# Twelve conditioning steps as blocks of 256 columns behind the small products of the heads

## The chip, the cores and the metric

The kernel runs on one core of a Trainium2 chip. The metric is device time in microseconds (us) of one execution. Five engines work side by side, each through its own list of instructions in order: TensorE (PE) multiplies, VectorE (DVE) and ScalarE (ACT) do elementwise work, GpSimd (POOL) a little of it, and SyncE (SP) issues most of the transfers (DMA) from memory.

## The reference, cut to what matters

One decoder layer on 520 tokens (a prompt of 512 and 8 samples of one token), width 1024. All is computed in float32.

```python
cs  = silu(c)                                   # one conditioning row for the prompt, 8 for the samples
mod = cs @ w_mod + b_mod                        # w_mod [1024, 6144]: six parts of 1024 columns
sh1, sc1, g1, sh2, sc2, g2 = split(mod, 6)      # parts 0 to 5
h = rmsnorm(x, norm1_g) * (1 + sc1) + sh1
u = h @ w_in                                    # q, f, i, og, xb, yb, ga, gb: 8 x 1024 columns
o_a = rmsnorm(hgrn2(q, f, i, S0)) * silu(og)    # 8 heads of 128, chunkwise recurrence
o_b = rglru(conv(xb)) * gelu(yb)
merged = sigmoid(ga) * (o_a @ w_branch_a) + sigmoid(gb) * (o_b @ w_branch_b)
x = x + g1 * (merged @ w_out)
h2 = rmsnorm(x, norm2_g) * (1 + sc2) + sh2
x = x + g2 * (square(relu(h2 @ w_ff1)) @ w_ff2)
y = rmsnorm(x, final_norm_g)
```

Parts 2 (g1), 3 (sh2), 4 (sc2) and 5 (g2) of mod are needed only from the out-projection on. They are what the change moves.

## The kernel before

Tokens lie along the columns in two halves of 260. Each 128 columns of a weight matrix are a tile of 1024x128 float32, 512 KB, which SP loads into one of four buffers of the pool `wst` (`_load_w`, L106; L104 for rows of w_mod). ACT casts it to fp32r (`whi`, L115), DVE subtracts to get the rest (`wlo`, L118), and PE makes 48 products of 128x260 from a tile (`products`, L157): 8 blocks of K, three combinations of high and low halves, two halves of the tokens. These are called the main products below. The buffer of a tile is free when DVE has made `wlo` from it.

`run` writes a list of steps, each with its weights and a function. `weights`, `ready_w` and `take_w` turn the list of weights into the order of loads and splits, some tiles ahead of their use. A scheduler then places the instructions of each engine by the times it reckons for them, by priorities (`urgent`, `together`) and by ties set by hand (`behind`). So the code's order isn't the program's order; that is read from the built program.

The heads come first. Two heads make a pair, (0,1), (2,3), (4,5), (6,7). For each head the tiles kf, kq, kg and kv are multiplied; for each odd head `heads_prompt` works out the products within chunks of the pair by levels b = 1, 2, 4, ..., 64. A level is 32 small products in narrow columns of PE (128x32 stationary; moving 64 wide at b=1, L661, 32 wide from b=2 to 16, L666; 16 products at b=32; 8 of 64x64 at b=64, L670, with the sample products L619 behind them). After each level DVE multiplies the operands X for the next (L682 four times after b=1, L678 twice after each other one), so a level waits for DVE, and main products stand between the levels. DVE also makes the RG-LRU recurrence (`rg_scans`) in that time. Then come the gates, the two branches, the out-projection and the MLP.

Conditioning parts 0 and 1 are made in a start-up block. Parts 2, 4, 3 and 5 are made in 16 steps: a step takes two blocks of 128 rows of w_mod, 1024 columns wide (two loads of 512 KB, not split), and makes 8 products of 128x32 by 128x256 in float32 (`mod_rows`, L403), summed in PSUM over four steps. After a part's fourth step ACT copies the sum (`mod_out`), and two products with an identity (`mod_cols`, L417) and an addition on DVE turn it into columns. `mod_step` puts one step behind each gate with j = 5, others after branch tiles by a share, and one after every second tile of the out-projection.

Of the kernel before, what the change touches and what calls it, by code (L numbers as in the profile page):

```python
# [6 lines left out]
F32 = mybir.dt.float32  # L7
# [4 lines left out]
OP = mybir.AluOpType  # L12
# [3 lines left out]
D = 1024  # L16
# [4 lines left out]
KO = D // 128  # L21
# [13 lines left out]
FIRSTS = 3  # L35
ROWS = "rows"
MARK = "mark"
PLAIN = 8
# [41 lines left out]
class Kernel:  # L80
# [19 lines left out]
    def _load_w(self, key, pool):  # L100
        src, r0, c0 = key[:3]
        st = pool.tile([128, KO, 128], F32, name="wst")
        if ROWS in key:
# [295 lines left out]

    def mod_rows(self, ps, k, w):  # L400

        for j in range(4):
            self.nc.tensor.matmul(ps[32 * j:32 * j + 32, :256], self.cT[:, k, :], w[:, 256 * j:256 * j + 256],  # L403
                                  start=k == 0, stop=k == KO - 1)

# [22 lines left out]
    def mod(self, part, k):  # L428

        w = [self.take_w(self.mod_key(part, k + n)) for n in range(2)]  # L430
        if k == 0:
            self.psm = self.ppt.tile([128, 512], F32, name="pt")
        for n in range(2):
            self.mod_rows(self.psm, k + n, w[n])
        if k == KO - 2:
            self.mod_open = part, self.modT[:, 8 * part:8 * part + 8], self.mod_out(self.psm), \
                self.n2g if part == 4 else None

    def modc(self, part, k):
# [103 lines left out]

    def head(self, h, first=None):
# [4 lines left out]
        q = self.head_q(X[:, 2], first[1] if first else self.gemm(kq, self.h)[:, :, :HALF])  # L549
        og = self.slot(self.hg, "e")  # L550
        if first:
# [80 lines left out]
    def heads_prompt(self, hs):  # L632
# [5 lines left out]
        a32 = self.hg.tile([128, 2, NC, 32], F32, name="a32", bufs=1)  # L638
        at = self.at

        def halves(x, b, n):
# [8 lines left out]
        while b < C:  # L650
            n = L // (2 * b)
            p = self.pps.tile([128, 512], F32, name="ps")
            with self.together():
                for e in range(2):
                    Q, K = X[:, e, 0], X[:, e, 1]
                    for c in range(NC):
                        if b == 1:
                            for j in range(4):
                                s, o = c * C + 32 * j, 256 * e + 64 * c
                                o = p[32 * j:32 * j + 32, o:o + 64].rearrange("p (x t) -> p x t", x=2)  # L660
                                nc.tensor.matmul(o, K[:, s:s + 32], X[:, e, 0::2, s:s + 32], start=True, stop=True)  # L661
                        elif b <= 32:
                            for j in range(0, 128, 32 if b < 32 else 64):
                                s, o = c * C + j, 128 * e + 32 * c
                                d = s if b < 32 else s + 32
                                nc.tensor.matmul(p[j:j + 32, o:o + 32], K[:, s:s + 32], Q[:, d:d + 32], start=True,  # L666
                                                 stop=True)
                        else:
                            s, o = c * C, 256 * e + 64 * c
                            nc.tensor.matmul(p[:64, o:o + 64], K[:, s:s + 64], Q[:, s + 64:s + 128], start=True,  # L670
                                             stop=True)
                if b == 64:
                    po = self.heads_sample(hs)
# [1023 lines left out]
    def run(self):  # L1697
# [28 lines left out]
        def mod_step(due):  # L1726
            if due < 0.999 or not mods:
                return due
            p, k = mods.pop(0)
            steps.append(([self.mod_key(p, k + n) for n in range(2)], self.mod, p, k))  # L1730
            return due - 1

# [3 lines left out]
        for h in range(H):  # L1736
            kf, kq, kv, kg = self.head_cols(h)
            steps.append(([kf, kq, kg, kv][FIRSTS if h == 0 else 0:], self.head_start if h == 0 else self.head, h))
# [16 lines left out]
        self.gate_out = {"a": ga, "b": gb}  # L1755
        share, due = (len(mods) - n - 2) / (2 * KO), 0.0
        last = len(self.gate_seq) - 1
        marks = [s for s, (u, j) in enumerate(self.gate_seq) if j in (1, 2)][:-1] + [last - 3, last - 1]
        for s, (u, j) in enumerate(self.gate_seq):
# [3 lines left out]
            if j == 5:  # L1763
                mod_step(1)
        steps.append(([], self.end_gates))
        tiles = [("b", m) for m in range(KO)] + [("a", m) for m in range(KO)]
        for g, m in tiles:
# [4 lines left out]
            else:  # L1772
                one("w_branch_a", m, lambda m: self.merge(m, ga.pop(m), gb.pop(m)), m)
            due = mod_step(due + share)
        steps.append(([], self.load_xT))
        steps.append(([], self.shifts))
        steps.append(([], self.begin_strassen))
        for m in range(KO):
            one("w_out", m, self.out_proj, m)
            if m % 2:  # L1780
                mod_step(1)
        assert not mods, mods
        steps.append(([], self.norm2))
# [306 lines left out]
```

## Time and profile before

| | |
|---|---|
| runs | 1012.15, 1014.35, 1015.53 us, median 1014.35 |
| profiled execution | 1014.92 us, its span 1013.1 us |
| PE, DVE, ACT, POOL busy | 993.7, 709.8, 529.4, 136.2 us |
| heads | about 60 to 442 us |
| gates | about 442 to 491 us |
| branches, out-projection | about 491 to 630 us, then the MLP |

All durations in the prediction are of the profiled execution; its own time stands 0.57 us above the median of the runs. In the groups of the profile a row has the line, the engine, the operation, out<-in, the shapes and the count, then busy time, the mean of one in ns, and the idle time just before it with what ended it. In the timeline a row has start and length in us. A matmul's length includes its way through the array, so matmuls that follow each other overlap, and what one costs the stream is read from starts. [...]

### The profile page before, as it was taken

The page shows a single profiled execution, that of the slowest core. Times are in us where ns is not written, and L with a number is a line of the kernel's source. Part 1 is how long each engine was busy: PE and PEld are TensorE (multiplying, and loading weights), DVE is VectorE, ACT ScalarE, POOL GpSimd, SP SyncE. Part 2 cuts the span into 40 slices and gives each one's busy share as a digit, 9 for nine tenths or more (in the row PEclk, how much of TensorE's full clock was granted, in tenths as well). Part 3 has the DMA queues.
Part 4 walks back from the last instruction along what each step waited for, and adds up shares of the span by engine and source line. Part 5 has one row for each costly group of instructions (what it writes and reads, how often), then busy time and mean ns, then how long its engine had stood idle before and what let it go on. Part 6 is the DMA issues. An engine that isn't in the chain of part 4 may idle for free. (4 is left out here: it accounts for less than half of the span.)

```text
span 1013.1 us, 23612 instructions
## 1 busy us (share of the span) xinstructions
PE 993.7 (98%) x9690; PEld 962.5 (95%) x9690; DVE 709.8 (70%) x1489; ACT 529.4 (52%) x1007; POOL 136.2 (13%) x261
## 2 busy tenths in 40 slices
PE   6999999999999999999999999999999999999997
PEld 5799999999989999998999999999999999999996
DVE  7586767695676669987723646667767776777685
ACT  6374645744663564455512224466555645646663
POOL 4220000000000000111100000022321331242050
PEclk7999999999999999999999999999999999999999
DMA  9883354345335435548357876332772483274242
GB/s 298 272 250 111 112 147 130 102 121 140 112 110 147 125 98 160 156 156 255 116 170 216 269 223 188 104 85 50 151 176 64 98 196 103 53 165 97 64 84 85
DMA packets 205278, 145.81 MB, mean 144 GB/s; under 512 B 6979, under 2 KB 193755, under 8 KB 205162
## 3 DMA queue, kind: packets, MB, share of 16 engines
q1 hardware_dynamic: 193586, 127.43, 43.0%
q0 software_dynamic: 11568, 16.84, 7.7%
q8 instruction: 76, 1.25, 0.5%
q14 instruction: 32, 0.26, 0.1%
q10 hardware_dynamic: 16, 0.03, 0.0%
HBM read 123.61 MB, written 13.39 MB: 135 GB/s over the span
## 5 line engine op out<-in xcount | busy, mean ns | idle before, releaser
L157 PE MATMUL mm<-h,whi 128*128 128x260 f32 (+1 forms) x2688 | 446.9, 285 | 0.0
L157 PEld LDWEIGHTS mm<-h,whi 128*128 128x128 f32 x2688 | 374.2, 189 | 1.5 <-issue 0.6
L157 PE MATMUL mm<-h,wlo 128*128 128x260 f32 x1344 | 276.5, 285 | 1.1 <-DVE wlo L118 1.1
L118 DVE TENSOR_TENSOR wlo<-wst,whi 128x1024 fp32r<-128x1024 f32 x156 | 190.5, 1222 | 113.4 <-ACT whi L115 108.0
L115 ACT CAST whi<-wst 128x1024 fp32r<-128x1024 f32 x156 | 163.5, 1050 | 187.7 <-PE mm L157 141.7
L157 PEld LDWEIGHTS mm<-h,wlo 128*128 128x128 f32 x1344 | 209.7, 189 | 2.2 <-DVE wlo L118 1.5
L916 POOL DMA_DIRECT2D t<-obT_d x8 | 4.3, 544 | 371.1 <-DVE g L745 365.5
L1421 DVE TENSOR_TENSOR f<-f 128x260 f32<-128x260 f32 x64 | 27.3, 427 | 27.9 <-ACT f L1416 27.2
L1413 POOL TENSOR_TENSOR ft<-ft,fsh 128x8 f32<-128x8 f32 x28 | 18.5, 659 | 207.4 <-DVE ft L1407 207.4
L1410 ACT ACTIVATE ft<-ft,fsh 128x512 f32<-128x512 f32 (+2 forms) x36 | 24.1, 676 | 36.0 <-DVE ft L1407 36.0
L157 PE MATMUL mm<-oa,whi 128*128 128x260 f32 x256 | 41.9, 285 | 0.0
L157 PE MATMUL mm<-a,whi 128*128 128x260 f32 x256 | 41.5, 284 | 0.0
L157 PE MATMUL mm<-b,whi 128*128 128x260 f32 x256 | 41.3, 284 | 0.0
L157 PEld LDWEIGHTS mm<-oa,whi 128*128 128x128 f32 x256 | 34.9, 188 | 2.1 <-ACT whi L115 1.2
L157 PEld LDWEIGHTS mm<-a,whi 128*128 128x128 f32 x256 | 35.0, 188 | 1.2 <-PE pt L403 0.8
L157 PEld LDWEIGHTS mm<-b,whi 128*128 128x128 f32 x256 | 34.9, 188 | 1.2 <-issue 0.8
L678 DVE TENSOR_TENSOR X<-X,tb 128x512 f32<-128x512 f32 x48 | 30.9, 685 | 4.1 <-PE ps L670 3.0
L1455 POOL DMA_DIRECT2D ma<-snap x28 | 27.6, 1001 | 38.5 <-issue 25.3
L1437 POOL DMA_DIRECT2D ma<-snap x28 | 27.0, 965 | 40.7 <-DMA ma<-snap 25.5
L1416 ACT ACTIVATE f<-ft 128x520 f32<-128x520 f32 (+1 forms) x36 | 20.8, 588 | 15.0 <-POOL ft L1414 13.0
L586 ACT ACTIVATE st<-st,fkq 128x128 f32<-128x128 f32 x64 | 19.8, 393 | 14.7 <-DMA st<-in_state_hgrn_dram 11.1
L1002 DVE TENSOR_TENSOR wgate<-gw,wgate 128x512 fp32r<-128x512 f32 x28 | 19.0, 689 | 11.1 <-ACT wgate L1001 11.0
(623 smaller groups left out, 2144.3 us busy)
## 6 DMA issues: line engine op xcount, KB each, us to landing
wst<-in_w_in_dram SPq DMA_DIRECT2D x56, 512.0 KB, 4.3
wst<-in_w_mod_dram SPq DMA_DIRECT2D x32, 512.0 KB, 4.1
wst<-in_w_ff_dram SPq DMA_DIRECT2D x64, 256.0 KB, 4.1
wst<-in_w_ff_dram SPq DMA_DIRECT2D x32, 512.0 KB, 5.1
wm<-in_w_mod_dram SPq DMA_DIRECT2D x8, 1024.0 KB, 10.7
st<-in_state_hgrn_dram SPq DMA_DIRECT2D x8, 512.0 KB, 6.8
vb<-vd SPq DMA_DIRECT2D x8, 512.0 KB, 3.8
out_dram<-st SPq DMA_DIRECT2D x8, 512.0 KB, 3.2
```

Of the source, the lines that this page charges most:

```text
L115: ins = self.nc.scalar.copy(hi, st)
L118: self.nc.vector.tensor_tensor(lo, st, hi.bitcast(F32), OP.subtract)
L157: self.last_product = self.nc.tensor.matmul(ps[s][:, :c.stop - c.start], x, y[:, c], start=first and n == 0, stop=last and n == 2)
L586: nc.scalar.activation(st[:, b], st[:, b], AF.Copy, scale=fkq[:, b:b + 1])
L678: last = nc.vector.tensor_tensor(half, half, factors(tbs, x, b), OP.mult)
L1002: nc.vector.tensor_tensor(lo, x, hi.bitcast(F32), OP.subtract)
L1410: nc.scalar.activation(t[:, :p], t[:, :p], AF.Relu, bias=sh[:, 0:1])
L1413: eng.tensor_tensor(t[:, p:], t[:, p:], sh[:, 1:9], OP.add)
L1416: nc.scalar.activation(f, self.two(self.ft)[:, a:a + n], AF.Square)
L1421: self.nc.vector.tensor_tensor(f[:, n], f[:, a], f[:, b], op)
L1437: nc.gpsimd.dma_start(x[1][:, b], v[:, :n], accum_op=OP.add)
L1455: nc.gpsimd.dma_start(x[t][:, a], s[p], accum_op=OP.add)
```

## The change

Parts 2, 4 and 3 become twelve units (`mod_unit`): four blocks of 256 columns for each part, each with all of K. A unit's weights are two tiles of 1024x128, loaded like other tiles (512 KB each) and not split; they keep their two buffers until the unit's last product. A unit makes 32 products of 128x32 by 128x64 (L459), a copy on ACT, two products of 128x64 by 64x18 (L468) and one or two operations on DVE (L475, L477). Its products are tied behind the last product of a level, `level_last[b]`, with b from `UNITS`. Three pairs have four units each: in pairs (0,1), (2,3) and (4,5) a unit stands after the odd head (b=1), one after the two rg_y tiles (b=4), one in the next even head after q (b=16) and one after that head (b=64). They are called U0 to U3, U4 to U7 and U8 to U11 here. Part 5 keeps its four steps, all behind the gates with j = 5. `ready_w` counts loaded tiles that are still held, instead of places in the list.

```diff
+UNITS = (1, 4, 16, 64)
...
-            while self.wnext_load < min(self.wnext_split + loads, len(self.worder)):
+            while self.wnext_load < len(self.worder) and self.staged() < loads:
...
+    def staged(self):
+        return max(sum(st is not None for st in self.wstage.values()), self.wnext_load - self.wnext_split - 8)
...
+    def mod_unit(self, u, b):
+
+        nc, (part, n) = self.nc, u
+        w = [self.take_w(key).rearrange("p (k n) -> p k n", k=KO) for key in self.unit_keys(u)]
+        pt = self.ppb.tile([128, 512], F32, name="pb")
+        with self.together():
+            for k in range(KO):
+                for j in range(4):
+                    x, e = divmod(j, 2)
+                    ins = nc.tensor.matmul(pt[32 * j:32 * j + 32, :64], self.cT[:, k, :],
+                                           w[e][:, k, 64 * x:64 * x + 64], start=k == 0, stop=k == KO - 1)
+                    self.behind(ins, self.level_last[b])
+        ev = self.sm.tile([128, 256], F32, name="modev")
+        with self.urgent():
+            nc.scalar.copy(ev[:, :64], pt[:, :64])
+        own = self.ident.rearrange("p (j c) -> p j c", c=32)[:, :, :NM]
+        with self.together():
+            for x in range(2):
+                ins = nc.tensor.matmul(pt[64 * x:64 * x + 64, 64:64 + 2 * NM].rearrange("p (e b) -> p e b", b=NM),
+                                       ev[:, :64], own[:, 2 * x:2 * x + 2], start=True, stop=True)
+                if 2 * b in self.level_last:
+                    self.behind(ins, self.level_last[2 * b])
...
-        mods = [(p, k) for p in (2, 4, 3, 5) for k in range(0, KO, 2)]
+        units = [(p, n) for p in (2, 4, 3) for n in range(4)]
+        mods = [(5, k) for k in range(0, KO, 2)]
...
+            if h and h % 2 == 0:
+                u = units[:2]
+                del units[:2]
+                steps.append(([kf, kq, *self.unit_keys(u[0]), kg, kv], self.head, h, None, u[0]))
+                steps.append((self.unit_keys(u[1]), self.mod_unit, u[1], UNITS[3]))
+            else:
+                steps.append(([kf, kq, kg, kv][FIRSTS if h == 0 else 0:], self.head_start if h == 0 else self.head, h))
+            if h % 2 and h < H - 1:
+                u = units.pop(0)
+                steps.append((self.unit_keys(u), self.mod_unit, u, UNITS[0]))
             for n in (h - 1, h) if h % 2 else (h, h + 1):
                 one("w_in", (40 if h % 2 else 32) + n, self.rg_y if h % 2 else self.rg_x, n)
+            if h % 2 and h < H - 1:
+                u = units.pop(0)
+                steps.append((self.unit_keys(u), self.mod_unit, u, UNITS[1]))
...
-            due = mod_step(due + share)
...
-            if m % 2:
-                mod_step(1)
```

The order of instructions shows where this lands. First, PE at the levels b=1 and b=2 of pair (2,3). L157 is a main product, L661 the level b=1, L628 transposes, L666 a level from b=2 on. Before:

```order
L661 MATMUL ps<-X_799 32x64 x32
L157 MATMUL mm<-h,whi 128x260 x2
L628 MATMUL pt<-ident,X_798 128x128 x4
L157 MATMUL mm<-h,wlo 128x260 x2
L157 MATMUL mm<-h,whi 128x260 x4
L157 MATMUL mm<-h,wlo 128x260 x2
L157 MATMUL mm<-h,whi 128x260 x4
L157 MATMUL mm<-h,wlo 128x260 x2
L666 MATMUL ps<-X_799 32x32 x32
```

After, where L704 is the level b=1, L710 a level from b=2 on, L162 a main product and L459 a product of U4:

```order
L704 MATMUL ps<-X_799 32x64 x32
L459 MATMUL pb<-wst,cT 32x64 x19
L710 MATMUL ps<-X_799 32x32 x16
L459 MATMUL pb<-wst,cT 32x64
L710 MATMUL ps<-X_799 32x32 x16
L459 MATMUL pb<-wst,cT 32x64 x12
L162 MATMUL mm<-h,whi 128x260
```

The 16 main products between the two levels are gone from there; 19 unit products stand in their place, and the rest of U4 stands around the halves of b=2.

Second, PE around the level b=16 of the same pair. Before, 37 main products stand between b=8 and b=16 and 33 behind it; a piece:

```order
L157 MATMUL mm<-h,whi 128x260 x4
L157 MATMUL mm<-h,wlo 128x260 x2
L157 MATMUL mm<-h,whi 128x260 x2
L666 MATMUL ps<-X_799 32x32 x32
L157 MATMUL mm<-h,whi 128x260 x2
L157 MATMUL mm<-h,wlo 128x260 x2
```

After, from the level b=8 to U6 (L468 are the column products of U5):

```order
L710 MATMUL ps<-X_799 32x32 x32
L459 MATMUL pb<-wst,cT 32x64 x23
L162 MATMUL mm<-h,whi 128x260 x4
L162 MATMUL mm<-h,wlo 128x260 x2
L162 MATMUL mm<-h,whi 128x260 x4
L162 MATMUL mm<-h,wlo 128x260 x2
L162 MATMUL mm<-h,whi 128x260 x4
L162 MATMUL mm<-h,wlo 128x260 x2
L162 MATMUL mm<-h,whi 128x260 x4
L468 MATMUL pb<-ident,modev 64x18 x2
L710 MATMUL ps<-X_799 32x32 x32
L459 MATMUL pb<-wst,cT 32x64 x32
```

Between b=8 and b=16 stand 23 products of U5, 22 main products and two column products; U6 follows b=16 directly, and 18 main products stand between it and b=32. From b=1 to b=64 the pair has 209 main products before and 151 after. On DVE the split of kf's tile stands in the new order directly ahead of the two operations L723 that make X after b=8, with two copies and one operation of the RG-LRU between them.

Third, the transfers that SP issues in that stretch, with what each waits for. Before:

```order
L776 DMA oaT_d_95<-e_1252 128x512 [waits DVE_49]
L106 DMA wst_3226<-in_w_in_dram 128x8x128 [waits DMAHW6_49,DVE_49]
L610 DMA out_5_dram<-st_2415 128x8x128 [waits DMAHW7_49,DVE_49]
L106 DMA wst_3286<-in_w_in_dram 128x8x128 [waits DMAHW0_49,DVE_49]
L885 DMA obT_d_96<-y_3150 128x520 [waits DMAHW1_49,DVE_49]
L106 DMA wst_3344<-in_w_in_dram 128x8x128 [waits DVE_49]
```

After, where wst_3307 is the second tile of U5, wst_3371 kf's and wst_3373 kq's tile of the next head, wst_3375 and wst_3480 the two tiles of U6, and wst_3540 kg's:

```order
L108 DMA wst_3307<-in_w_mod_dram 128x8x128 [waits PE_49]
L108 DMA wst_3371<-in_w_in_dram 128x8x128 [waits DMAHW7_49,PE_49]
L652 DMA out_5_dram<-st_2583 128x8x128 [waits DMAHW0_49,DVE_49]
L108 DMA wst_3373<-in_w_in_dram 128x8x128 [waits DMAHW1_49,DVE_49]
L108 DMA wst_3375<-in_w_mod_dram 128x8x128 [waits DMAHW7_49,DMAHW2_49,DVE_49]
L108 DMA wst_3480<-in_w_mod_dram 128x8x128 [waits PE_49]
L108 DMA wst_3540<-in_w_in_dram 128x8x128 [waits DMAHW6_49,DMAHW4_49,PE_49]
```

Before, each load waits for the split of an earlier tile. After, wst_3307 and wst_3371 wait for the last product of U4 on PE, wst_3375 for the split of kf's tile on DVE, and wst_3480 and wst_3540 for the end of U5.

More of the change, by code (lines that the diff above doesn't have):

```diff
@@ L36 @@
 ROWS = "rows"
+UNIT = "unit"
+UNITS = (1, 4, 16, 64)
 MARK = "mark"
@@ L102, in _load_w @@
         st = pool.tile([128, KO, 128], F32, name="wst")
-        if ROWS in key:
+        if ROWS in key and UNIT not in key:
             self.nc.sync.dma_start(st.rearrange("p k n -> p (k n)"), src[r0:r0 + 128, c0:c0 + 1024])
@@ L398, in mod_key, with mod_rows @@
         return (self.i["w_mod"][0], k * 128, part * D, ROWS)
-    def mod_rows(self, ps, k, w):
+    def mod_rows(self, ps, k, w, after=None):
         for j in range(4):
-            self.nc.tensor.matmul(ps[32 * j:32 * j + 32, :256], self.cT[:, k, :], w[:, 256 * j:256 * j + 256],
-                                  start=k == 0, stop=k == KO - 1)
+            ins = self.nc.tensor.matmul(ps[32 * j:32 * j + 32, :256], self.cT[:, k, :], w[:, 256 * j:256 * j + 256],
+                                        start=k == 0, stop=k == KO - 1)
+            if after:
+                self.behind(ins, after)
     def mod_out(self, ps):
@@ L437, in mod, with unit_keys @@
                 self.n2g if part == 4 else None
+    def unit_keys(self, u):
+        part, n = u
+        return [(self.i["w_mod"][0], 0, part * D + 256 * n + 128 * e, ROWS, UNIT) for e in range(2)]
+    def mod_unit(self, u, b):
[19 more added lines that the diff above has]
+                    self.behind(ins, self.level_last[2 * b])
+        out = self.modT[:, 8 * part + 2 * n:8 * part + 2 * n + 2]
+        src = pt[:, 64:64 + 2 * NM].rearrange("p (e b) -> p e b", b=NM)
+        col = lambda c: c[:, :, None].to_broadcast([128, 2, NM])
+        nc.vector.tensor_tensor(out, src, col(self.bmod[:, part * 8 + 2 * n:part * 8 + 2 * n + 2]), OP.add)
+        if part == 4:
+            nc.vector.tensor_tensor(out, out, col(self.n2g[:, 2 * n:2 * n + 2]), OP.mult)
     def modc(self, part, k):
@@ L542, in head_q, with head @@
         return q
-    def head(self, h, first=None):
+    def head(self, h, first=None, unit=None):
         nc = self.nc
@@ L549, in head @@
         q = self.head_q(X[:, 2], first[1] if first else self.gemm(kq, self.h)[:, :, :HALF])
+        if unit:
+            self.mod_unit(unit, UNITS[2])
         og = self.slot(self.hg, "e")
@@ L1779, in run @@
             one("w_out", m, self.out_proj, m)
-            if m % 2:
-                mod_step(1)
-        assert not mods, mods
+        assert not mods and not units, (mods, units)
         steps.append(([], self.norm2))
```

23 lines of the change are left out of this document (11 added, 12 removed).

## The prediction

> **What bounds the kernel now.** I read the busy times first, then the windows by stage, then what TensorE (PE) waited for. The page's first part:
>
> ```profile
> PE 993.7 (98%) x9690; PEld 962.5 (95%) x9690; DVE 709.8 (70%) x1489; ACT 529.4 (52%) x1007; POOL 136.2 (13%) x261
> ```
>
> PE is busy 98% of the span, so an instruction taken from it is worth its time, unless a wait takes its place. The windows (start:end, length, then busy time of each engine) cover the heads (60 to 442 us), one pair's level stretch inside them, the gates, and branches with out-projection:
>
> ```profile
> 60.00:442.00 382.00, 378.56 (x4498) 370.56 (x4498) 284.95 (x706) 208.51 (x435) 3.80 (x7) 1.00 0.44 129
> 194.00:232.00 38.00, 37.12 (x643) 35.35 (x643) 32.57 (x70) 20.40 (x30) 0.00 (x0) 1.00 0.43 129
> 442.00:491.00 49.00, 48.33 (x420) 43.24 (x418) 36.31 (x71) 29.19 (x60) 5.38 (x10) 1.00 0.66 205
> 491.00:630.00 139.00, 1.79 (x14) 1.68 (x13) 1.00 0.69 207
> ```
>
> PE stands idle 382 - 378.56 = 3.44 us in the heads and 0.67 us in the gates. The last row is the same window for the column products L417 alone; PE had no idle time in it at all. The engine that comes next in the heads is VectorE (DVE): 32.57 of 38 us, 86%, in a level stretch, where it makes the operands X of each next level, the RG-LRU scans and the low halves of the weights. What PE waited for in the heads:
>
> ```profile
> PE mm L157 <- DVE wlo L118: 1.1, 1, 1.1
> PE ps L666 <- DVE X L682: 0.7, 1, 0.7
> PE pt L628 <- DVE e L775: 0.6, 1, 0.6
> ```
>
> All three are DVE. So the change has to be costed twice: the PE time of steps and units, and the waits on DVE and on loads that a new order leaves uncovered.
>
> **What goes.** One old step in the timeline (start, length, then engine, line, tile, count), between main products:
>
> ```profile
> 589.84 0.41 PE L157 MATMUL mm<-oa,wlo 128*128 128x260 f32 x2
> 590.17 1.07 PE L403 MATMUL pt<-wst,cT 128*32 128x256 f32 x16
> 591.18 0.75 PE L157 MATMUL mm<-oa,whi 128*128 128x260 f32 x4
> ```
>
> Main products start 0.12 us apart (two in 0.41 us, of which the last takes 0.29 us). Without the step the next one would start at 589.84 + 2 x 0.12 = 590.08; it starts at 591.18, and its group of four takes 0.75 instead of 0.65 us. A step costs 1.10 + 0.10 = 1.20 us. Twelve: 14.4 us.
>
> The five steps near the gates cost more, since other products stand between their parts. The step's line in the two windows, and its row among the groups:
>
> ```profile
> 442.00:485.00 43.00, 6.98 (x80) 2.59 (x80) 1.00 0.75 233
> 485.00:630.00 145.00, 12.39 (x176) 4.72 (x176) 1.00 0.66 199
> L403 PE MATMUL pt<-wst,cT 128*32 128x256 f32 x256 | 19.4, 385 | 0.7 <-DMA wst<-in_w_mod_dram 0.7
> ```
>
> Eleven unbroken steps have 12.39/11 = 1.13 us of busy time each; five near the gates have 6.98, which is 6.98 - 5 x 1.13 = 1.35 more, and 0.7 of waiting for weights. The four steps that stay stand unbroken in the new order, so I let 2.05 us go (0 if they break again).
>
> Three of four column products L417 go:
>
> ```profile
> 490.07 0.76 PE L1028 MATMUL ps<-a,wgate 128*128 128x260 f32 x5
> 490.67 0.53 PE L417 MATMUL pb<-ident,modev 128*128 128x36 f32 x4
> 491.03 0.72 PE L157 MATMUL mm<-b,whi 128*128 128x260 f32 x4
> ```
>
> Next product due at 490.67, started at 491.03, and its four are 0.07 late: 0.43 us each, 1.3 in all. Removed: 14.4 + 2.05 + 1.3 = 17.75 us.
>
> **What comes, on PE.** A unit has 32 products of 128x32 stationary by 128x64 moving, 64 records. The level b=1 (L661) is exactly that shape and count:
>
> ```profile
> 105.97 0.28 PE L815 MATMUL pb<-xcs,bdhlru_wx 128*128 128x260 f32 x1
> 106.18 1.10 PE L661 MATMUL ps<-X 128*32 128x64 f32 x64
> 107.21 0.39 PE L815 MATMUL pb<-xcs,bdhlru_wx 128*128 128x260 f32 x1
> 107.44 0.29 PE L815 MATMUL pb<-xcs,bdllru_wx 128*128 128x260 f32 x1
> ```
>
> By itself it delays the stream by 107.21 - 106.09 = 1.12, and 0.11 behind it: 1.23 us. Inside, with 0.22 us for the last record, records start (1.10 - 0.22)/63 = 14 ns apart, 0.89 us for 64. So entering and leaving narrow columns costs about 0.33 us. A unit directly behind a level pays 0.89, one between main products 1.23. The two column products L468 (64x18) have no row of their own: lower bound 0.13 behind a level, 0.43 (as L417) by themselves; I take those two values by place.
>
> By the order, pair (2,3) and likewise (4,5) has four units behind levels, 3.56, less 0.33 since b=2 no longer enters by itself, and two L468 by themselves, two merged, 1.12: 4.4 us. Pair (0,1) has one unit alone and one cut by transposes: 2 x 0.89 + 2 x 1.23 = 4.24, and L468 three alone and one merged, 1.4: 5.6 us. Added: 14.4 us. Net on PE 14.4 - 17.75 = -3.3 us (-1 with broken gate steps, -4.5 with cheaper L468).
>
> [...]
>
> **What comes off PE.** Unit copies (ACT, 128x64) and adds (DVE, 128x18) are behind no main product; ACT is at 208.5 of 382 us. What counts are three waits.
>
> (1) Level b=2, pairs (2,3) and (4,5). Before, 16 main products and a transpose covered VectorE's four X operations; now 19 unit products stand there.
>
> ```profile
> 194.00 1.10 PE L661 MATMUL ps<-X 128*32 128x64 f32 x64
> 196.03 1.43 DVE L682 TENSOR_TENSOR X<-X,ma 128x256 f32<-128x256 f32 x4
> ```
>
> The last L661 starts at 194.88, X begins 1.15 us later, two of four are ready at about 196.03 + 0.34 + 0.42 = 196.79, 1.91 us after L661. PE is there after 38 records x 14 ns = 0.53: it stands 1.4 us, and about 0.3 more before the second half, which needs all four. 1.65 us twice: 3.3 (0 if VectorE begins directly behind L661, 5 if it comes as late again as here).
>
> (2) Unit loads. A unit's weights are two 512 KB tiles, and four buffers serve all. In pair (2,3) the second tile of U6 waits for U5's last product, and behind it in SP's queue stand the tiles of kg and kv, which PE needs only after U6. The first tile waits ahead of both for kf's buffer, free when VectorE has split kf (wlo), directly ahead of the X operations of b=8.
>
> ```profile
> L678 DVE TENSOR_TENSOR X<-X,tb 128x512 f32<-128x512 f32 x48 | 30.9, 685 | 4.1 <-PE ps L670 3.0
> 198.44 0.76 PE L666 MATMUL ps<-X 128*32 128x32 f32 x64
> 199.14 0.75 PE L157 MATMUL mm<-h,whi 128*128 128x260 f32 x4
> wst<-in_w_in_dram SPq DMA_DIRECT2D x48, 512.0 KB, 4.1
> st<-in_state_hgrn_dram SPq DMA_DIRECT2D x7, 512.0 KB, 6.7
> ```
>
> From U5's end to U6 PE has 22 main products (2.64), a merged L468 (0.13) and a level (0.7): 3.5 us. A load lands in 4.1 by itself, so U6 stands 0.6 us at least; the state loads, issued two in a row like these, took 6.7, so 3.2. The first tile has less time where VectorE sets the pace: two X operations (1.3) and the level (0.7), 2.0 us, so 6.7 - 2.0 = 4.7 at most. I take 2.2, below the middle, since VectorE need not set the pace there; two pairs: 4.4 us.
>
> [...]
>
> (3) Less cover between levels. By the order, 209 main products stood between b=1 and b=64 in pair (2,3), now 151: 58 x 0.12 = 7.0 us fewer, and U4 to U6 with their L468 bring about 3.1. The chain is 3.9 us shorter for nearly the same work of an engine that has 5.4 us of idle time in 38. Between 0 and 3.9 I take 0.7 a pair, most of it fitting into that idle time: 1.4. In pair (0,1) main products stand ahead of each unit, and only U3's second load, which waits for U2's end some 5 us ahead, comes close to 4.1 to 6.7: 1.0 (0 to 3).
>
> Of before's 3.44 us, about 0.7 lie outside these stretches and stay. Waits after: 3.3 + 4.4 + 1.4 + 1.0 + 0.7 = 10.8 us, 7.4 more. Sum: -3.3 + 7.4 = +4.1 us. The span is 1013.1, the profiled execution 1014.92 us; it becomes 1019.0. Against the median of three, 1014.35, it is 1018.4 us. From the gates on the order of main products is unchanged, and PE has no idle time there to give.
>
> **Rivals.** A difference of 0.3%, 3.0 us, is about what the spread of the three runs allows to tell.
>
> *Waits don't grow* (22%). VectorE has fewer splits in the shorter stretch and starts X directly behind L661, and what is left of its waits at b=16 gives U6's loads their time. Then only the net on PE counts, and the waits at L666 and L628, which stood at these places, go: -3.3 - 1.3 = -4.6, 1009.7 us. For it: ACT and DVE have idle time in each window. Against it: DVE at 86%, and all three large waits of before are DVE's. It decides at b=2 and U6: waits under 0.4 us at both.
>
> *Only b=2 waits* (20%), and U6 by its least, 0.6 us twice: -4.6 + 3.3 + 1.2 = -0.1, 1014.2 us, no change that can be told.
>
> *Loads decide* (15%). Every unit load stands behind another unit's end, so U5 and U7 wait too: U6 at 4.7 twice, U5 and U7 1 us each twice, U3 3 us. Waits are 3.3 + 9.4 + 4 + 1.4 + 3 + 0.7 = 21.8, 18.4 more, and the time 1014.35 - 3.3 + 18.4 = 1029.4 us; with U5 and U7 in time 1025. Against it: a pair's units are 25 to 50 main products apart, 3 to 6 us.
>
> **How the numbers follow.** The forecast, waits at b=2 and at U6 of middle size, has 43%: 1018.4 us, its own range 1014 to 1023. It and the last rival are slower by over 0.3%, above 1017.4, except for some 5% of the forecast's lower end: 0.53. Within 0.3% are the second rival and that lower end, less what falls on the faster side: 0.24. Faster, below 1011.3: 0.23. The range, from the first rival to the milder form of the last: 1009.5 to 1025.
>
> **What would show it.** Right: PE idle at L710 b=2 by 1.3 to 2 us with VectorE X as what ended it; PE idle at L459 with a load of w_mod ending it in pairs (2,3) and (4,5); L459 in narrow columns at 14 ns a record; no idle time from 491 us on. Wrong: idle time in the heads below 5 us (then the first or second rival), units that cost over 1.3 us without a wait, or gate steps broken as before (2 us worse than summed).

## The result, and the profile after

The changed kernel takes 1030.33 us (median of four runs, 1027.74 to 1032.52) against 1014.25 us for the kernel before on the same chip: 1.0157 times as long, interval 1.0129 to 1.0186. The prediction was 1018.4 with a range up to 1025.0: the sign was right, the size was not. The profiled execution, the fastest of the four, took 1027.74 us, its span 1025.9.

New lines: b=1 is L704, b=2 to 32 L710, b=64 L714, the unit's products L459 and L468, its copy L464, the step's products L408, main products L162, gate products L1073 with weights from ACT (L1046) and DVE (L1047).

The page's first part of the changed kernel, and its windows for the heads (60 to 468 us), the gates and the start of the branches, with busy time of PE, PEld, DVE, ACT and POOL, then granted clock, DMA share and GB/s:

```profile
PE 994.2 (97%) x10302; PEld 971.1 (95%) x10302; DVE 709.6 (69%) x1501; ACT 529.5 (52%) x1016; POOL 135.3 (13%) x261
60.00:468.00 408.00, 395.69 (x5296) 385.09 (x5295) 281.56 (x716) 206.84 (x442) 3.83 (x7) 0.99 0.53 150
468.00:520.00 52.00, 48.75 (x415) 45.16 (x414) 37.51 (x71) 30.48 (x61) 5.38 (x10) 0.97 0.55 170
520.00:660.00 140.00, 139.82 (x1164) 139.11 (x1164) 83.52 (x137) 45.31 (x60) 10.36 (x21) 1.00 0.51 141
```

PE's busy time hardly changed (993.7 before). Its idle time did: 408 - 395.69 = 12.31 us in the heads (3.44 before) and 3.25 in the gates (0.67 before). And the granted clock is below 1.00 in both. What PE waited for between 60 and 640 us (total, times, longest; the seven largest rows of thirteen):

```profile
PE pb L459 <- DMA wst<-in_w_mod_dram: 5.5, 4, 1.4
PE mm L162 <- issue: 1.5, 1, 1.5
PE pb L468 <- ACT modev L464: 1.5, 3, 0.5
PE mm L1073 <- DVE wgate L1047: 1.2, 1, 1.2
PE mm L1073 <- ACT gp L1084: 1.0, 1, 1.0
PE mm L1073 <- ACT wgate L1046: 1.0, 1, 1.0
PE pb L459 <- issue: 1.0, 1, 1.0
```

The units' loads come first, as predicted. But "issue", the unit's own chain (L468 behind the copy) and three waits in the gates stand in no term of the sum.

By stage, from starts in the timeline (first b=1 record, first and last gate product, first product of the MLP's second matrix, L1318 before and L1363 after), against the prediction's terms (heads: 14.4 of PE and 7.4 of waits; gates: one step of 1.20 and the 2.05 gone; branches: eleven steps and three column products gone):

| stage | before | after | change | predicted |
|---|---|---|---|---|
| start to b=1 of pair (0,1) | 106.2 | 103.2 | -3.0 | 0 |
| b=1 to the first gate product | 336.6 | 365.0 | +28.4 | +21.8 |
| gate products | 50.2 | 52.1 | +1.9 | -3.25 |
| branches, out-projection, first matrix of the MLP | 204.8 | 190.6 | -14.2 | -14.5 |
| rest of the MLP | 315.4 | 315.0 | -0.3 | 0 |

The start-up differs between the profiled executions of this case (first b=1 record at 103.2 to 111.4 us; half clock ahead of it for 13.7 us in the kernel before and 3.4 in the changed one), and I don't count it as the change's. Without it the change costs +15.8 us against +4.1 predicted: 6.6 us more in the heads, 5.2 more in the gates.

Where the heads lose it: PE in pair (2,3), from b=1 through U5 to U6 and b=32:

```profile
200.89 1.10 PE L704 MATMUL ps<-X 128*32 128x64 f32 x64
202.71 0.46 PE L710 MATMUL ps<-X 128*32 128x32 f32 x32 [0.16 <-ACT g L625]
...
215.94 0.85 PE L459 MATMUL pb<-wst,cT 128*32 128x64 f32 x45
218.29 0.75 PE L162 MATMUL mm<-h,whi 128*128 128x260 f32 x4 [1.50 <-issue]
...
222.25 0.27 PE L459 MATMUL pb<-wst,cT 128*32 128x64 f32 x2
223.95 0.89 PE L459 MATMUL pb<-wst,cT 128*32 128x64 f32 x35 [1.43 <-DMA wst<-in_w_mod_dram]
225.80 1.06 PE L459 MATMUL pb<-wst,cT 128*32 128x64 f32 x27 [0.96 <-issue]
...
227.40 1.07 PE L162 MATMUL mm<-h,whi 128*128 128x260 f32 x4
```

Behind U5 PE stands 1.50 us though the profile names nothing that it waits for; U6 starts with two records and stands 1.43 us for a tile; in the middle of U6 it stands 0.96 us more; and then four main products take 1.07 us, which took 0.75. The last is the clock, in windows of 2 us:

```profile
222.00:224.00 2.00, 0.43 (x19) 0.19 (x10) 1.73 (x3) 1.17 (x2) 0.00 (x0) 1.00 1.18 292
226.00:228.00 2.00, 2.00 (x32) 1.83 (x25) 0.52 (x2) 0.58 (x2) 0.00 (x0) 0.50 0.09 28
228.00:230.00 2.00, 2.00 (x12) 2.00 (x11) 1.78 (x3) 0.73 (x2) 0.00 (x0) 0.50 0.84 243
```

PE was busy 0.43 of the 2 us before 224; from about 224.4 to 231.2 its clock was granted at one half. In the kernel before no window of the heads was below 1.00. The 18 main products in it start about 0.22 instead of 0.12 us apart, 1.75 us, and with the rest of U6 and b=32 I estimate 2.4 us lost.

The other engines at this place (SP's queue, DVE, ACT):

```profile
218.09 0.99 SPq L108 DMA_DIRECT2D wst<-in_w_mod_dram  x2
216.85 1.21 DVE L120 TENSOR_TENSOR wlo<-wst,whi 128x1024 fp32r<-128x1024 f32 x1
219.25 0.19 ACT L464 COPY modev<-pb 128x64 f32<-128x64 f32 x1
```

U6's two loads go out at 218.09, directly behind the wlo that ends at 218.06: the buffer of kf, as the prediction had it. The copy of U5, whose products end at 216.8, runs only at 219.25, since ACT's list is in order and the operation ahead of it waited 3.22 us for DVE. The same loads at U10 in pair (4,5) and at U3 in pair (0,1):

```profile
323.28 0.27 PE L459 MATMUL pb<-wst,cT 128*32 128x64 f32 x2 [1.23 <-DMA wst<-in_w_mod_dram]
324.94 1.09 PE L459 MATMUL pb<-wst,cT 128*32 128x64 f32 x62 [1.39 <-DMA wst<-in_w_mod_dram]
...
140.26 0.77 PE L459 MATMUL pb<-wst,cT 128*32 128x64 f32 x40 [1.44 <-DMA wst<-in_w_mod_dram]
```

And the gates:

```profile
477.18 1.07 PE L408 MATMUL pt<-wst,cT 128*32 128x256 f32 x16
485.19 0.51 PE L1073 MATMUL mm<-a,wgate 128*128 128x260 f32 x2 [1.00 <-ACT wgate L1046]
486.92 2.29 PE L1073 MATMUL mm<-a,wgate 128*128 128x260 f32 x10 [1.22 <-DVE wgate L1047]
489.01 2.34 PE L1073 MATMUL pb<-h,wgate 128*128 128x260 f32 x12
```

The steps stand unbroken, as said. But two products between two waits for gate weights leave PE nearly idle for 3 us, and the next 22 products run at half clock: 10 in 2.09 us and 12 in 2.18 instead of 22 x 0.12 = 2.64, 1.6 us lost.

### The profile page after: what moved, and what is told of

Its sections match the earlier page's. It is cut to its first block, busy times and chain, and to the rows that moved or that the text cites. A ratio compares the mean times of both kernels' runs of the same rounds, so it can differ in the third digit from the quotient of the medians.

```text
span 1025.9 us, 24846 instructions
## 1 busy us (share of the span) xinstructions
PE 994.2 (97%) x10302; PEld 971.1 (95%) x10302; DVE 709.6 (69%) x1501; ACT 529.5 (52%) x1016; POOL 135.3 (13%) x261
## 5 line engine op out<-in xcount | busy, mean ns | idle before, releaser
L162 PE MATMUL mm<-h,whi 128*128 128x260 f32 (+1 forms) x2688 | 446.9, 285 | 1.5 <-issue 1.5
L162 PEld LDWEIGHTS mm<-h,whi 128*128 128x128 f32 x2688 | 375.3, 189 | 2.5 <-issue 1.7
L162 PE MATMUL mm<-h,wlo 128*128 128x260 f32 x1344 | 279.3, 286 | 0.9 <-DVE wlo L120 0.9
L162 PEld LDWEIGHTS mm<-h,wlo 128*128 128x128 f32 x1344 | 210.8, 189 | 2.6 <-DVE wlo L120 1.3
L162 PE MATMUL mm<-b,whi 128*128 128x260 f32 x256 | 41.3, 283 | 0.1
L162 PE MATMUL mm<-oa,whi 128*128 128x260 f32 x256 | 41.3, 283 | 0.0
L162 PE MATMUL mm<-a,whi 128*128 128x260 f32 x256 | 41.1, 283 | 0.0
L162 PEld LDWEIGHTS mm<-b,whi 128*128 128x128 f32 x256 | 35.0, 188 | 0.4 <-ACT whi L117 0.4
L723 DVE TENSOR_TENSOR X<-X,tb 128x512 f32<-128x512 f32 x48 | 30.9, 684 | 6.5 <-PE ps L710 4.3
L162 PEld LDWEIGHTS mm<-a,whi 128*128 128x128 f32 x256 | 35.1, 189 | 0.0
L162 PEld LDWEIGHTS mm<-oa,whi 128*128 128x128 f32 x256 | 34.9, 188 | 0.0
L162 PE MATMUL mm<-oa,wlo 128*128 128x260 f32 x128 | 25.8, 283 | 0.1
L162 PE MATMUL mm<-a,wlo 128*128 128x260 f32 x128 | 25.8, 283 | 0.0
```

The lines of the kernel that those rows point to most:

```text
L162: self.last_product = self.nc.tensor.matmul(ps[s][:, :c.stop - c.start], x, y[:, c], start=first and n == 0, stop=last and n == 2)
L723: last = nc.vector.tensor_tensor(half, half, factors(tbs, x, b), OP.mult)
```

## Experiments

All times are medians, the ratio against the kernel before on the same chip (medians 1013.1 to 1015.9). The chips differ between some of the rows, so rows are best compared by their ratios. e2, e3, e4, e6, e7 and e10 leave out part of the computation. For each, the heads (first b=1 record to first gate product) and the gates (first to last gate product) of its profiled execution:

| kernel | us | ratio and interval | heads | gates |
|---|---|---|---|---|
| before (first profile) | 1014.25 | | 336.6 | 50.2 |
| after | 1030.33 | 1.0157 (1.0129 to 1.0186) | 365.0 | 52.1 |
| e1_untied | 1031.83 | 1.0158 (1.0129 to 1.0187) | 365.1 | 53.2 |
| e2_resident | 1027.02 | 1.0095 (1.0066 to 1.0123) | 360.1 | 50.6 |
| e3_resident_untied | 1022.98 | 1.0069 (1.0047 to 1.0090) | 359.0 | 52.5 |
| e4_resident_wide | 1018.37 | 1.0044 (1.0022 to 1.0066) | 355.1 | 50.0 |
| e5_doubled | 1028.75 | 1.0140 (1.0113 to 1.0167) | 346.9 | 54.4 |
| e6_nochain | 1015.09 | 1.0016 (0.9992 to 1.0041) | 351.0 | 51.7 |
| e7_onestep | 1026.45 | 1.0125 (1.0093 to 1.0157) | 365.7 | 49.1 |
| e8_one_pair | 1023.45 | 1.0108 (1.0070 to 1.0145) | 347.6 | 53.5 |
| e9_early_steps | 1030.79 | 1.0157 (1.0122 to 1.0192) | 365.6 | 51.5 |
| e10_no_b16 | 1012.83 | 0.9974 (0.9948 to 1.0001) | 349.9 | 49.4 |
| e11_three_each | 1043.12 | 1.0281 (1.0246 to 1.0317) | 380.5 | 46.1 |
| e12_b32 | 1023.73 | 1.0104 (1.0082 to 1.0125) | 361.5 | 51.9 |

**The tie of the gate steps (e1_untied).**

```diff
-            self.mod_rows(self.psm, k + n, w[n], self.last_product)
+            self.mod_rows(self.psm, k + n, w[n])
```

> The four steps of part 5 lose their tie to the last gate product; all else as in the changed kernel. Theory 'gates': the old steps were filler in the time in which the gates wait for wgate, and tied they are not; 3.2 us of waits between 471 and 487 us and about 1.1 us of half clock behind them go, 1030.3 becomes about 1026 us, and PE waits for wgate under 1 us. Rival: the gates are late because their loads are late (SP holds the gw loads behind the steps' loads): the waits stay and the time stays within 1 us of 1030.3.

PE's waits in this kernel, the row that took the place of those for the gate weights:

```profile
PE pt L408 <- DMA wst<-in_w_mod_dram: 3.7, 1, 3.7
```

Nothing is gained. Without the tie the products of two steps run together, and the fifth tile isn't there yet. The tie isn't what costs the gates their 5 us.

**The units' loads (e2_resident, e3_resident_untied).** The units multiply a tile that is on the chip all the time (the identity), so no unit load is issued and no buffer held; e3 has this and the edit of e1.

```diff
-        return [(self.i["w_mod"][0], 0, part * D + 256 * n + 128 * e, ROWS, UNIT) for e in range(2)]
+        return []
...
-                                           w[e][:, k, 64 * x:64 * x + 64], start=k == 0, stop=k == KO - 1)
+                                           self.ident[:, :64], start=k == 0, stop=k == KO - 1)
```

> The units read a resident identity in place of their weights (their 24 loads are left out, so parts 2 to 4 are wrong); products, copies and ties as in the changed kernel. Theory 'loads': 5.5 us of waits for w_mod tiles go, and with them most of the half clock behind (about 2.4 us) and the waits of kf's tile: 1030.3 becomes 1020 to 1022 us. Rival 'instruction fetch': a level and a unit behind it are 128 records, 256 instructions in 1.8 us, and PE runs out of instructions; then waits named issue stay at L459 and behind it, 2 to 3 us, and the time is 1024 to 1026 us.

> Both edits of the two runs before: no unit loads, and steps without the tie. If the two causes add, 1016 to 1018 us, near the time before; if the gates' waits come only from the heads being late, no better than the run without loads. By the forecast's PE sum alone, without any new wait, it would be 1011 us.

PE's waits at the units in e2 (L457 is its L459):

```profile
PE pb L457 <- DVE modT L473: 3.3, 3, 1.7
PE pb L457 <- issue: 1.3, 1, 1.3
```

The load waits of 5.5 us are gone, and the heads are 4.9 us shorter, still 23.5 longer than before. The median of e2 lies above both expectations (six runs, 1020.9 to 1029.4). In the loads' place stands DVE's addition L473, which reads the unit's sum out of PSUM: the unit behind it waits until the tile is free. So loads are a part only; take them away and the next chain ends last. e3, at 1022.98, missed its 1016 to 1018: its heads are 1.1 us shorter than e2's, and its gates gain nothing, since a step there waits 2.9 us for its load.

**The number of products (e4_resident_wide).** As e3, but a unit is 16 products of 128 columns instead of 32 of 64 (half of K is left out): the same columns streamed, half the instructions.

```diff
-            for k in range(KO):
+            for k in range(KO // 2):
...
-                    ins = nc.tensor.matmul(pt[32 * j:32 * j + 32, :64], self.cT[:, k, :],
+                    ins = nc.tensor.matmul(pt[32 * j:32 * j + 32, :128], self.cT[:, k, :],
```

> As the run with both edits, but a unit is 16 products of 128 columns in place of 32 of 64 (half of K left out): the same time in the array, half the instructions. Theory 'instruction fetch': waits named issue behind units go and it is 2 to 4 us faster than the run with both edits. Rival: PE has its instructions in time; the two are within 1 us.

No wait named "issue" and no half clock was left in the heads, which became 3.9 us shorter than e3's; the median fell by 4.6 us. That speaks for the supply of instructions; the run doesn't isolate it, since the order in pairs (2,3) and (4,5) shifted a little too.

**Levels twice, no units (e5_doubled).** The kernel before, with the small products of b=1 to 16 of three pairs issued twice: PE time added behind the levels, in the same narrow form, with no load, PSUM tile or copy.

```diff
-                for e in range(2):
+                for e in range(2) if b > 16 or hs[1] == H - 1 else (0, 1, 0, 1):
```

> The kernel before, with the products of levels b=1 to 16 of the first three pairs issued twice, directly behind each other; no unit, no load, no copy is added. By PE alone 3 x 0.89 + 12 x 0.6 = 9.9 us more. Theory 'instruction fetch': each doubled level is 128 records, 256 instructions without a main product between, and in about a quarter of them PE stands 1.5 to 1.8 us for instructions, with an idle named issue: 14 to 17 us more in all, half clock behind some. Rival: narrow products cost what they cost, 9 to 11 us more and no such idle.

Its waits, and one of the places in its timeline:

```profile
PE mm L157 <- issue: 3.8, 2, 2.2
```

```profile
110.26 1.60 PE L666 MATMUL ps<-X 128*32 128x32 f32 x128
...
114.06 0.28 PE L157 MATMUL mm<-h,whi 128*128 128x260 f32 x1 [1.52 <-issue]
```

The heads grew by 10.3 us. That is near the 9.9 of computed PE time by chance: PE's busy time there rose by 8.2 us (333.4 to 341.6) and its idle time by 2.1. "issue" appears where 128 narrow records follow each other, with no unit in the program (a third one, 0.6 us, stands at L666). So that wait needs no unit; here it stands behind 128 short records in a row. The rest of its +14 us lies in the gates (+4.2), where the steps wait 3.0 us for their weights although nothing was edited there; why, is open.

**The chain behind a unit (e6_nochain).** As e3, without the copy, the products L468 and the additions (columns 16 to 39 of modT hold a constant).

> As the run with a resident operand and untied steps (1023.0 us), but a unit is its 32 products alone: no copy on ACT, no L468, no addition on DVE (parts 2 to 4 are constants). L468 on PE cost 4 us by the forecast (1.1 + 1.1 + 1.4 and the merged ones). Theory 'chain': the next unit waits, in the one PSUM tile, for the copy, the column products and the addition of the unit before (3.3 us for DVE modT, 1.3 for ACT modev), so 8 us go: 1015 us. Rival: these waits stand in for others (X of the level, fetch), and only L468's own 4 us go: 1019 us.

The heads are 8.0 us shorter than e3's, of which the prediction's price of L468 is 1.4 + 1.12 + 1.12 = 3.6; the other 4.4 are waits and half clock (3.4 us of it in e3's heads, none here): `modT` and `modev` are gone from the list, "issue" is still there with 2.4 us. So the chain through one PSUM tile (copy late in ACT's list, L468, addition on DVE) is the second part.

**The gates (e7_onestep, e9_early_steps).** e7 leaves three of part 5's four steps out (the lines that then end the sum after one step aren't shown); e9 moves the first two of the four steps behind the gates s = 1 and 6.

```diff
-        mods = [(5, k) for k in range(0, KO, 2)]
+        mods = [(5, 0)]
```

```diff
-            if j == 5:
+            if s in (1, 6) or j == 5 and u > 1:
```

> The changed kernel with one of the four gate steps (the other three and their six loads are left out, so part 5 is wrong). Theory 'filler': gates are paced by their own weights (loads of gw, casts on ACT, splits on DVE), steps fill waits, and without three of them the time stays within 1.5 us of the changed kernel. Rival: steps cost their 1.2 us each, 3.6 us less.

> The changed kernel, but the first two of the four gate steps stand behind the 2nd and the 7th gate product, where PE waited 1.0 and, a little later, 2.2 us for gate weights; the last two as before them. Theory 'gates begin behind their weights': a step there fills a wait, so 2 to 3.5 us go, with the half clock behind the second wait: 1030.3 becomes 1026 to 1028 us. Rival: the gate weights are made only when PE frees their buffers; the waits move behind the steps and the time stays.

In e7, then in e9:

```profile
PE mm L1073 <- DVE wgate L1047: 1.4, 1, 1.4
PE mm L1073 <- ACT gp L1084: 1.0, 1, 1.0
PE mm L1073 <- ACT wgate L1046: 0.9, 1, 0.9
```

```profile
PE mm L1073 <- ACT b L216: 3.3, 1, 3.3
```

Three steps out shorten e7's gates by 3.0 us, about their PE time; its waits stay. So those three steps neither hide these waits nor cause them. In e9 one wait of 3.3 us takes the place of the three. ACT's rows in that window say that its cast L216 waited 5.0 us for a transfer (`t<-obT_d`; 1.7 before, without harm to PE). What makes the gates' operands late is left open.

**One pair of units only (e8_one_pair).** Part 2 is made by units in pair (0,1), the other parts by the steps of before. The tie of the steps is left out as in e1. The first lines of the edit; the others put the units in pair (0,1) alone and the steps at their old places:

```diff
-        units = [(p, n) for p in (2, 4, 3) for n in range(4)]
-        mods = [(5, k) for k in range(0, KO, 2)]
+        units = [(2, n) for n in range(4)]
+        mods = [(p, k) for p in (4, 3, 5) for k in range(0, KO, 2)]
```

> Part 2 alone as four units in pair (0,1); parts 4, 3 and 5 as twelve steps at the places of the kernel before. If each pair with units costs alike and the gates keep their five steps as filler, a third of the heads' 14 us is lost and 5.2 us of steps are gained: before + 4 to 5 us with the units' 5.6 us of PE. If the three pairs hinder each other (loads of one late for the next), before + 0 to 2 us.

It came out 10.3 us above the kernel before, some 5 us above the higher of the two expectations. From b=1 to b=1, pair (0,1) grew by 9.8 us, (2,3) shrank by 3.6, (4,5) grew by 4.8 with no unit in it, and in the gates two steps wait 5.9 us for their weights. The effect reaches far behind the place that is edited, so this run doesn't price a pair.

**The units at b=16 (e10_no_b16).** U2, U6 and U10 are left out with their six loads (their columns hold a constant); nine units stay.

```diff
-                steps.append(([kf, kq, *self.unit_keys(u[0]), kg, kv], self.head, h, None, u[0]))
+                steps.append(([kf, kq, kg, kv], self.head, h))
```

> The changed kernel without the three units at b=16 (U2, U6, U10) and their six loads; a quarter of parts 2 to 4 is a constant. On PE 3 x 0.89 + 3 merged L468 of 0.13 to 0.43, 3.5 us, go in any case. Theory 'loads at b=16': the waits for w_mod tiles at U6 and U10 (4.0 us), the half clock behind (2.4) and the wait for instructions there (1.0) go too: 1019 to 1021 us. Rival: the four buffers are short anywhere, and other units or main products wait instead: 1025 to 1027 us.

The window of its heads, and three of its waits there:

```profile
60.00:448.00 388.00, 383.46 (x5044) 373.74 (x5043) 280.11 (x679) 206.80 (x422) 5.50 (x15) 1.00 0.53 151
PE ps L711 <- DVE X L728: 1.2, 2, 1.0
PE pb L469 <- ACT modev L465: 0.8, 2, 0.5
PE ps L711 <- issue: 0.3, 1, 0.3
```

This is the largest single effect, 6 us more than expected: 17.5 us for about 3.5 us of PE by the prediction's prices (three units of 0.89 and their L468). In the heads 15.1 us go: 8.0 of idle time and 7.1 of busy time, of which half clock is about 2.4. The gates, where nothing was edited, lose 2.7 us too, with 2.0 us of idle time in place of 3.25 and no half clock. No wait for a w_mod tile is left, at U3 neither, and the clock stays at 1.00. The other nine units keep their ties, and all idle time is 4.5 us, 1.1 more than before. The scheduler did move some of them: U5 now runs as one group of 64 records ahead of the level b=8, with main products between, so what e10 saves isn't the three units alone.

**Other places for them (e11_three_each, e12_b32).** e11 takes the b=16 units out of the heads of three pairs and puts three units behind the last pair's levels, with e9's steps; e12 moves them from b=16 to b=32.

```diff
-                steps.append(([kf, kq, *self.unit_keys(u[0]), kg, kv], self.head, h, None, u[0]))
-                steps.append((self.unit_keys(u[1]), self.mod_unit, u[1], UNITS[3]))
+                steps.append(([kf, kq, kg, kv], self.head, h))
+                steps.append((self.unit_keys(u), self.mod_unit, u, UNITS[3]))
...
+            if m < 3:
+                u = units.pop(0)
+                steps.append((self.unit_keys(u), self.mod_unit, u, (4, 16, 64)[m]))
```

```diff
-UNITS = (1, 4, 16, 64)
+UNITS = (1, 4, 32, 64)
```

> All twelve units, none at b=16: the three that stood there come behind the heads, ahead of the gates, each between main products; steps as in the early-step run. If both theories hold, 1030.3 less 7 at b=16 and 3 in the gates, more 1 us for units that stand alone: about 1021 us, still slower than before. If the waits move along with the units, 1026 to 1030.

> The changed kernel with one number changed: UNITS = (1, 4, 32, 64), so the third unit of a pair is tied behind b=32 in place of b=16. In pairs (2,3) and (4,5) 86 main products then stand between U5 and U6 (22 before) and 45 between U6 and U7. Theory 'spacing': what costs at b=16 is that two units stand 22 main products apart, less than a tile's load, the chain through the one PSUM tile and a fetch of instructions need; with 86 the waits at U6 and U10 and the half clock behind go, and it is 1012.8 (the run without these units) plus 3.5 to 5 us for the three units: 1016 to 1018 us. Rival 'number': four units a pair hold too many buffers wherever they stand; the waits move to U7 and to the main products, 1025 us or more.

The worst wait of e11, its window there, and the first two rows of e12's waits:

```profile
PE pt L799 <- DVE g L790: 6.8, 1, 6.8
430.00:480.00 50.00, 35.02 (x404) 32.70 (x405) 28.06 (x76) 18.55 (x47) 7.08 (x13) 0.80 0.56 167
```

```profile
PE pt L786 <- ACT g L781: 3.1, 3, 1.6
PE pb L459 <- DVE modT L475: 2.0, 2, 1.0
```

e11 missed; as I read it, too few main products stand behind the last pair to cover a unit's chain. PE is busy 35 of 50 us, at a clock of 0.80, 12.8 us over the changed kernel. e12 is 6.6 us faster than the changed kernel (5.4 by the ratios), between its two expectations; with e8 (1.0108) it is the least slow of the versions with the whole computation. No w_mod tile is late at its units, and "issue" is down to 0.3 us. It is still 1.0104 times the kernel before: its heads are 24.9 us longer, 7.7 of it idle time, in which PE now waits for ACT, DVE and the PSUM tile. No version with the whole computation beat the kernel before.

## Why the prediction was wrong in size

**What goes** held: branches and out-projection lost 14.2 us for 14.5 summed. At the gates the broken steps did become whole, so the 2.05 went, but it did not show. The sum had no term for new waits there: 2.6 us more idle time and about 1.6 at half clock, and the stage grew by 1.9 instead of shrinking by 3.25. The step that failed there is the sentence that from the gates on the order is unchanged and has no idle time to give. The order of products was unchanged; the state in which ACT, DVE and the transfers reach the gates was not. That this state comes from the heads is borne out by e5 and e10: both edit the heads alone, and their gates take 4.2 us more than before and 2.7 us less than the changed kernel's. What of it ends last isn't settled.

**What comes, on PE** held for a unit by itself: U5 has its 45 records in 0.85 us, 14 ns apart. The sum was too small, though: PE's busy time from b=1 to the gates rose by 19.3 us (333.4 to 352.7), of which about 2.4 is half clock, so 16.9 for 14.4 reckoned. e12, whose heads ran at full clock, says the same with 17.2. In e5 the same way of reckoning gave 9.9 for 8.2. Records of 256 columns in an old step start (1.07 - 0.38)/15 = 0.046 us, 46 ns, apart, per column about the same as the 14 ns for 64. The price of 0.13 us for L468 behind a level was the author's estimate, which no row gave: U5's L468 starts at 221.13 and the level behind it at 221.35, 0.22 later.

**(1) b=2** was too dear: PE starts the level with 0.16 us of waiting, 202.71 - 200.89 = 1.82 us behind the start of b=1, where the sum had 1.65 us of standing still. The sum took DVE's late start from the kernel before, 1.15 us behind the last record of b=1; there DVE still had `e` (L775) to make. Now X begins together with that last record (200.89 + 0.88 = 201.77), the lower end of the term's own range:

```profile
201.68 1.44 DVE L727 TENSOR_TENSOR X<-X,ma 128x256 f32<-128x256 f32 x4
```

**(3) Less cover** was too dear too: with (1) it had 4.7 us, and all waits of PE at the levels L710 and L714 are 1.3 us.

**(2) U6's loads** was right in its price and wrong in being the whole price. Load waits were 1.43 us in pair (2,3) and 1.23 + 1.39 in (4,5), 4.05 in all for 4.4 predicted; (3)'s U3 cost 1.44 for 1.0. (PE had U6's second tile 5.4 us after its issue at 218.51; the prediction's rows had 4.1 and 6.7.) The step that failed in the heads is "What counts are three waits", with the unit's copy and addition put at nothing because no main product stands behind them. At U5 and U6 came what no term had: "issue" 1.50 + 0.96, and 2.4 at half clock behind it; and at the units of b=1 L468 stood behind its copy, three times 0.5 us. All idle time in the heads rose by 8.9 us for 7.4 predicted, the clock took 2.4, and 28.4 - 14.4 - 8.9 - 2.4 = 2.7 us are the busy time beyond the sum, which no row places. A unit that a wait breaks enters narrow columns anew, at 0.33 us by the prediction's row; five such breaks would be 1.6. So the miss of 6.6 us in the heads is 1.5 of idle time, 2.4 of clock and 2.7 of busy time; the idle time is as near as that only because (1) and (3) were 3.4 us too dear, which is luck. e10 prices the place: without the units at b=16 the heads are 15.1 us shorter and the kernel 17.5, where the sum had 3.5 of PE, 4.4 and 1.0 for them.

Most of it belongs to this place. From U5's last product to U6 there are 22 main products and a level, 3.4 us. In that time U6 needs two loads, of which the second took 5.4 us, the PSUM tile that U5's copy, L468 and addition must free, and its instructions. The prediction followed the first. e2 took the loads away, and e6 and e4, built on it, the chain and half the instructions; each time others stood there: 4.9, 8.0 (3.6 of it PE) and 3.9 us. That it isn't the place alone, e12 shows: at b=32 the same units cost 5 to 7 us less, not 17.5.

**The rivals.** *Waits don't grow* and *Only b=2 waits* fell with the first row of waits. *Loads decide* named 1029.4 us and came nearest, by luck: U5 and U7, its premise, were in time, and loads took 5.5 us, not 16.4.

## What to carry to other kernels

A step that is moved needs more than its PE time and its loads: list all that it shares with its last user (weight buffers, the PSUM tile, the in-order list of the engine that empties it, the run of instructions ahead of it) and compare each with the time between the two. Where several are late at one place, taking one away shows little, and leaving out the whole work of that place prices it at once, as e10 did where e2, e4 and e6 showed parts. And waits close together on a dense PE had a tail of half clock here: 6.8 us of it, behind 3.41 us in which PE was busy for 1.84.

## What the runs showed of the hardware

**The supply of instructions.** From the page's DMA queues of the changed kernel, and the same view for 214 to 232 us (packets, MB, share):

```profile
q8 instruction: 81, 1.33, 0.5%
q8 instruction: 3, 0.05, 1.1%
```

PE and PEld have 2 x 10302 records, 254 for each of the 81 packets if all of them are theirs, which no row says. A level and a unit are 4 x 64 = 256 records; those of b=8 and U5 start within 1.8 us (215.02 to 216.79). PE then stood 0.4 to 2.2 us with nothing named as late (after, e1, e2, e3, e5, e6, e7, e9), and did not in e4. Not every such run stops PE: behind U9, with the same 45 records in a row, it went on at once (317.15 + 0.85 us, the next main product at 317.93). In the changed kernel a packet of q8 starts at 215.92 and one at 223.34 us, and PE goes on at 218.29 and 225.80, 2.37 and 2.46 us later; the heads have 41 of these packets in 408 us, one in 10 us. No row names the packet as the releaser, so that PE waited for instructions is a reading of these times, not shown.

**The clock.** It fell to 0.50 at about 224.4 and at 487.2 us, each time after some 3 us with PE partly busy, for 6.83 and 3.41 us. PE's busy time in the 3.41 us ahead of each:

```profile
221.00:224.41 3.41, 1.84 (x104) 1.00 1.17 303
483.83:487.24 3.41, 1.19 (x8) 1.00 0.49 190
```

So PE needn't stand idle for the whole stretch: it was busy for 1.84 and 1.19 us of it. The four changes of the clock between 60 and 1000 us in this execution, at 224.41, 231.24, 487.24 and 490.65, lie 6.83, 256.00 and 3.41 us apart, 2, 75 and 1 times 3.413. Of the pieces of that length counted off from these points between 60 and 1000 us, the emptiest one at full clock that no fall follows, 319.97 to 323.39, had PE busy for 1.96 us. A long wait alone brought no fall in two other runs: behind the waits of 2.6 us in e4's gates and of 3.3 us in e8's the clock stayed at 1.00. What decides it, these runs don't show.
